# One pass over the weights for both column segments, three features held back, in a two-layer diffusion trunk

## The chip, the core and the metric

The kernel runs on one core of a Trainium2 chip. Its engines work side by side, each through its own queue in order: TensorE (matmuls; PE and, for its weight loads, PEld in the profile), VectorE (DVE), ScalarE (ACT), GpSimd (POOL) and SyncE (SP), which issues the DMAs. The metric is the time of one execution on the device, in microseconds (us), as the median of several runs.

## The reference

Two layers of a token mixer and a gated feed-forward network (FFN) over 512 latent tokens and 256 context tokens, all with 1024 features. The second layer needs the context only as keys and values.

```
for l in range(2):
    hl, hc = modulate(rmsnorm(xl), sh1, sc1) @ w_in[l], ...   # latent, context
    (four groups of heads: differential, windowed, neighbourhood attention, short convolution)
    xl = xl + g1 * (heads_l @ w_out[l])
    xl = xl + g2 * conv_ffn(modulate(rmsnorm(xl), sh2, sc2), w_up[l], ..., w_down[l])
    if l == 0:
        xc = xc + cg1 * (heads_c @ w_out[l])
        xc = xc + cg2 * conv_ffn(modulate(rmsnorm(xc), csh2, csc2), ...)
return rmsnorm(xl, final_norm_w)

conv_ffn: u = dwconv3(h @ w_up, conv_w) + conv_b;  g, v = split(u);  (silu(g) * v) @ w_down
```

All is float32. The kernel splits each operand of a matmul in a high part (rounded to the matmul's format) and a low part, the rest, and multiplies high by high, high by low and low by high: three matmuls for each tile of 128 input features.

## The kernel before

**Layout.** Features lie on the 128 partitions, in 8 tiles (`KT = 8`), tokens along the columns: 0 to 511 latent, 512 to 767 context. `x[m]` is the residual stream of feature tile m in SBUF, `y[k]` the normed input of the next product, with a high part `yh` and a low part `yl`. In layer 0 the two segments (`SEGS`) are the 512 latent and the 256 context columns; in layer 1, where the context is no longer needed, they are two halves (`HALVES`) of 256.

**Weights.** `prefetch` (L453) loads the next weight tiles in the order that `unit_order` (L433) yields, into 3 raw buffers; `split_weights` (L472) has ScalarE cast the high part (L481) and subtracts the low part (L486): on GpSimd in pieces of two tiles, or, with `fast`, the first five tiles on VectorE and the rest on GpSimd. There are two buffers for each part (`wh`, `wl`), and with `spare` two of another pool (`mrow`), which also takes the rows for the modulation sums of `mod_dve` (L304) during layer 0's FFN.

**The four stages that the change touches.** Stage 1 is layer 0's output projection with the norm before the FFN, stage 2 layer 0's last part of the down-projection (7 of 22 tiles) with the norm before layer 1's mixing, stage 3 and stage 4 the same two places of layer 1, where stage 4 ends in the final norm and the output. In each the weights are gone over twice, once for each segment: in `w_out` (L921) and in the loop over `sweeps` in `ffn` (L961). A product goes into one of two PSUM banks (`tp`), and VectorE adds it into x (`residual`, L914).

**The norm of a segment** is a generator: `rstd_steps` (L327) squares x on ScalarE and sums over features, then takes the root and the reciprocal, then spreads the result over all partitions by four small matmuls (`rb`, into the one PSUM bank tagged `pj`). For the second segment (`direct`) the sums over the eight tiles are made on TensorE, by matmuls with ones into the bank `pv` (`ms`); for the first, GpSimd and VectorE add the eight squares (L353) and TensorE sums once. Then `norm_apply` (L396) takes each feature tile k: VectorE multiplies x by the scale and by `rb`, straight from its bank (L404, called the first step below), ScalarE adds the shift and rounds to the high part (L408), and the low part is made on VectorE for even k (L414, the lower part) or on GpSimd for odd k (L410, L412).

**What sets the order.** A list scheduler orders each engine's instructions by its own estimate of when they are ready and by program order. `keep_in_program_order` pins an instruction behind the one traced just before it on its engine. `tick(n)` (L372) advances the norm in `self.pace` by n steps between the products of the other segment, and the first steps of features made under it are pinned (L406). `woven` (L379) runs the second segment's norm and, after each of its steps, one fill: products of the first segment with the weights of the two units that come next (`up_open`, or `early_start` in stage 2). While fills run, all of TensorE's matmuls are pinned, the broadcast of the root among them. The unit's results lie in the two `sc` tiles of PSUM.

In stage 1 the woven part is

```
first = [self.up_open(l, 0, gv, True) for gv in range(2)]
part = lambda u, k0, k1: lambda: self.up_product(u[1], u[0], y, a, b, range(k0, k1))
self.woven(steps, part(first[0], 0, 4), part(first[0], 4, 8), part(first[1], 0, 8))
```

so that the sums of the second norm come first, then half of unit 0, the last sum, the other half of unit 0, the broadcast, and unit 1.

After stage 2 the pools of the FFN are closed, and those of the mixing (`mixing_pools`, L249) take their memory; the first load into one of them is the table for the rotation (L588).

## Time and profile before

| what | value |
|---|---|
| median of 3 runs | 1758.03 us (1757.46 to 1758.92) |
| profiled execution: its time, its span | 1758.37 us, 1756.6 us |
| busy, share of the span: TensorE, its weight loads | 95%, 81% |
| VectorE, ScalarE, GpSimd | 54%, 46%, 57% |
| DMA moved | 244.15 MB, mean 139 GB/s |
| loads of w_out tiles, of w_down tiles of 448 KB, of 512 KB | 32, 48, 16 |

A busy share is a mean over stages with different limits, and TensorE's busy time counts matmuls that run slowly as busy. So the four stages are read one by one: how many matmuls fall in a stretch, what they take elsewhere, and what ended the waits. The window view gives, for a stretch, the busy time of each engine with its instructions, and the clock that was granted to TensorE as a share of 2.4 GHz.

### The profile page before, as it was taken

The numbers are of one execution on the slowest core, as the hardware profiler recorded it, in microseconds if no ns is written. First come the engines' busy times: TensorE is split into PE (matmuls) and PEld (weight loads), VectorE is DVE, ScalarE is ACT, GpSimd is POOL, SyncE is SP. The second block draws the span as 40 slices with busy tenths as digits, with TensorE's granted clock in tenths as the row PEclk, the third lists the DMA queues.
The fourth block names the chain that finished last, engine by engine and source line by source line (L and its number), as shares of the span: only waits on it lengthen the run. The fifth ranks groups of instructions, "written<-read, shape, count | busy, mean of one in ns | idle before, by whom it ended". The sixth has DMA issues, their size and how long they took to land. (4 is left out here: it accounts for less than half of the span.)

```text
span 1756.6 us, 26615 instructions
## 1 busy us (share of the span) xinstructions
PE 1672.1 (95%) x9740; PEld 1421.0 (81%) x9740; DVE 952.0 (54%) x1849; ACT 801.0 (46%) x1399; POOL 1002.0 (57%) x1348
## 2 busy tenths in 40 slices
PE   6899999899999999999999988999999999999997
PEld 4578878798878888888888877888879888888887
DVE  3577767562667754654355475877656422122245
ACT  4276766553443321332143354776654543242343
POOL 1424234776566654664467664434865776676763
PEclk9999999999999999999999999999999999999999
DMA  8566535336434433443333636453446323233334
GB/s 335 177 197 210 157 108 186 94 121 233 149 104 129 123 109 98 133 127 111 110 131 116 196 120 189 138 148 105 141 128 210 109 96 94 99 94 99 96 108 132
DMA packets 78450, 244.15 MB, mean 139 GB/s; under 512 B 9072, under 2 KB 12656, under 8 KB 78192
## 3 DMA queue, kind: packets, MB, share of 16 engines
q1 hardware_dynamic: 78320, 242.46, 43.6%
q8 instruction: 77, 1.26, 0.3%
q14 instruction: 53, 0.43, 0.1%
HBM read 214.64 MB, written 27.79 MB: 138 GB/s over the span
## 5 line engine op out<-in xcount | busy, mean ns | idle before, releaser
L486 POOL TENSOR_TENSOR wl<-raw,wh 128x256 fp32r<-128x256 f32 (+1 forms) x750 | 579.9, 803 | 556.1 <-ACT wh L481 528.5
L73 PE MATMUL pu<-y,wh 128*128 128x512 f32 (+1 forms) x1792 | 559.2, 388 | 4.2 <-DVE up L957 2.6
L481 ACT CAST wh<-raw 128x1024 fp32r<-128x1024 f32 (+1 forms) x228 | 233.6, 1027 | 353.8 <-PE pd L73 188.7
L73 PEld LDWEIGHTS pu<-y,wh 128*128 128x128 f32 x1792 | 331.8, 188 | 71.2 <-ACT wh L481 2.4
L73 PE MATMUL pu<-y,wl 128*128 128x512 f32 (+1 forms) x1072 | 369.0, 351 | 0.0
L73 PE MATMUL pj<-y,wh 128*128 128x512 f32 (+1 forms) x1216 | 325.4, 356 | 8.9 <-ACT ev L581 5.3
L73 PE MATMUL pd<-g,wh 128*128 128x512 f32 (+1 forms) x1048 | 290.2, 362 | 4.4 <-DVE x L917 2.8
L73 PEld LDWEIGHTS pj<-y,wh 128*128 128x128 f32 x1216 | 206.9, 192 | 39.1 <-ACT ev L581 8.2
L73 PEld LDWEIGHTS pu<-y,wl 128*128 128x128 f32 x1072 | 201.9, 188 | 31.1
L73 PEld LDWEIGHTS pd<-g,wh 128*128 128x128 f32 x1048 | 188.5, 193 | 34.2 <-ACT wh L481 4.0
L73 PE MATMUL pj<-y,wl 128*128 128x512 f32 (+1 forms) x608 | 212.0, 349 | 0.0
L954 DVE SCALAR_TENSOR_TENSOR up<-pu,par,up 128x511 f32<-128x511 f32 (+1 forms) x132 | 83.1, 658 | 231.4 <-ACT up L952 212.9
L73 PE MATMUL pd<-g,wl 128*128 128x512 f32 (+1 forms) x584 | 196.2, 342 | 2.9 <-DVE wl L486 2.8
L917 DVE SCALAR_TENSOR_TENSOR x<-pd,mod,x 128x256 f32<-128x256 f32 (+1 forms) x96 | 56.6, 592 | 168.9 <-PE pd L73 168.3
L73 PEld LDWEIGHTS pj<-y,wl 128*128 128x128 f32 x608 | 116.7, 192 | 14.5
L677 POOL TENSOR_TENSOR p<-p,rec 128x512 f32<-128x512 f32 (+2 forms) x80 | 79.5, 998 | 83.2 <-DVE rec L673 59.5
L73 PEld LDWEIGHTS pd<-g,wl 128*128 128x128 f32 x584 | 112.6, 193 | 17.3 <-DVE wl L486 3.5
L311 DVE SCALAR_TENSOR_TENSOR junk<-mrow,cbc 128x1024 f32<-128x1024 f32 x80 | 121.9, 1524 | 2.1 <-DMA mrow<-in_wmodt 1.3
L73 PE MATMUL po<-og,wh 128*128 128x256 f32 (+1 forms) x512 | 111.6, 314 | 3.9 <-ACT sq L344 2.5
L979 POOL TENSOR_TENSOR up<-up 128x256 f32<-128x256 f32 x105 | 105.3, 1028 | 1.4 <-DVE up L957 0.7
L748 DVE TENSOR_TENSOR wtl<-wtp,wth 128x512 fp32r<-128x512 f32 x132 | 87.4, 668 | 29.5 <-ACT wth L747 28.7
L73 PEld LDWEIGHTS po<-og,wh 128*128 128x128 f32 x512 | 84.8, 193 | 10.2 <-ACT sq L344 2.7
(174 smaller groups left out, 2370.8 us busy)
## 6 DMA issues: line engine op xcount, KB each, us to landing
raw<-in_wup SPq DMA_DIRECT2D x88, 512.0 KB, 3.4
mrow<-in_wmodt SPq DMA_DIRECT2D x56, 512.0 KB, 3.7
raw<-in_win SPq DMA_DIRECT2D x44, 512.0 KB, 3.6
raw<-in_wdn SPq DMA_DIRECT2D x48, 448.0 KB, 3.3
mraw<-in_wmod SPq DMA_DIRECT2D x40, 512.0 KB, 7.2
raw<-in_wout SPq DMA_DIRECT2D x32, 512.0 KB, 3.5
qk<-hl SPq DMA_DIRECT2D x16, 768.0 KB, 3.6
stk<-qk SPq DMA_DIRECT2D x32, 384.0 KB, 5.4
```

Of the source, the lines that this page charges most:

```text
L73: i = self.nc.tensor.matmul(out, **kw)
L311: self.tc.keep_in_program_order(nc.vector.scalar_tensor_tensor(out=junk, in0=raw, scalar=1.0, in1=self.cbc[:, i], op0=ALU.mult, op1=ALU.mu ...
L481: i = nc.scalar.copy(out=wh, in_=raw)
L486: eng.tensor_tensor(out=wl[:, a:b], in0=raw[:, a:b], in1=f32v(wh[:, a:b]), op=ALU.subtract)
L677: self.nc.gpsimd.tensor_tensor(out=p, in0=p, in1=r.broadcast_to(list(p.shape)), op=ALU.mult)
L748: nc.vector.tensor_tensor(out=wl[:, :n * 256], in0=tp[:, :n * 256], in1=f32v(wh[:, :n * 256]), op=ALU.subtract)
L917: self.nc.vector.scalar_tensor_tensor(out=x[m][:, a:b], in0=p[:, c:c + n], scalar=gate[:, m, (0 if b <= SEQ else 1):(1 if b <= SEQ else 2) ...
L954: nc.vector.scalar_tensor_tensor(out=u[:, a + 1:b], in0=p[:, a:b - 1], scalar=cw[:, 0:1], in1=u[:, a + 1:b], op0=ALU.mult, op1=ALU.add)
L979: eng.tensor_tensor(out=uv[:, a:b], in0=ug[:, a:b], in1=uv[:, a:b], op=ALU.mult)
```

## The change

`HELD = 3`. Each of the four stages goes over its weights once (`sweep`). For the first five feature tiles both segments are multiplied right away: in layer 0 as 512 and 256 columns, in layer 1 as one product of all 512. For the last three only the first segment is, and the weights are kept (the last tile's in the spare buffers). Then the first segment's norm starts, and the three held products of the second segment follow, with one step of the norm after each. Then the second segment's squares and sums are traced, then the next two units are opened (their weights split), then the rest of the first norm (`tick(KT + 2)`). The second norm is woven with fills of one feature tile each, for both units in turn. Both norms sum on TensorE (`direct` is True) and put their broadcast in `pj`. `norm_apply` takes one tile and returns its lower part as a function, which `norm_steps` calls two tiles later; under `tick` the lower parts are pinned too. All other stages are as before; the opening norm of the kernel calls the lower parts after each pair of tiles. In stage 2 the eight stores of x for layer 1 (L236) are traced after the early products instead of between the passes.

```diff
@@ -190,22 +192,21 @@
                 i = nc.sync.dma_start(out=x[m][:, :NT], in_=xsrc[:, m, :NT])
                 if m == 0:
                     tc.keep_in_program_order(i)
-            y = None
-            for sg in segs:
-                self.w_out(l, s, x, sg)
-                y = y or self.new_y()
-                steps = self.norm_steps(x, y, sg, self.affn[l], self.mod[l][:, 24:32], sg != segs[0])
-                if sg == segs[0]:
-                    self.pace = steps
-                    self.tick(1)
-            first = [self.up_open(l, 0, gv, True) for gv in range(2)]
+            y = []
+
+            def norm(sg, l=l, x=x, y=y, segs=segs):
+                y.extend([] if y else self.new_y())
+                return self.norm_steps(x, y, sg, self.affn[l], self.mod[l][:, 24:32], True, "pj")
+
+            steps, first = self.sweep(lambda m: ("wout", l, m), "po", s, x, self.mod[l][:, 16:24], segs, norm,
+                                      lambda: [self.up_open(l, 0, gv, True) for gv in range(2)])
             a, b = segs[0]
-            part = lambda u, k0, k1: lambda: self.up_product(u[1], u[0], y, a, b, range(k0, k1))
-            self.woven(steps, part(first[0], 0, 4), part(first[0], 4, 8), part(first[1], 0, 8))
+            part = lambda k: lambda: [self.up_product(u[1], u[0], y, a, b, range(k, k + 1)) for u in first]
+            self.woven(steps, *[part(k) for k in range(KT)])
             a, b = segs[1]
             self.pin = ALL
             for u in first:
-                part(u, 0, 8)()
+                self.up_product(u[1], u[0], y, a, b)
             self.pin = None
             todo = []
             if need:
...
@@ -216,29 +217,30 @@
 
-            def after(sg, l=l, need=need, x=x, y2=y2):
-                if need:
-                    if not y2:
-                        self.scale_vec(l + 1, self.amix[l + 1], O_NM, 8)
-                        y2.extend(self.new_y())
-                    steps = self.norm_steps(x, y2, sg, self.amix[l + 1], self.mod[l + 1][:, 0:8], sg != segs[0])
-                    if sg == segs[0]:
-                        self.pace = steps
-                        self.tick(1)
-                    else:
-                        early = self.early_start(l + 1, True)
-                        part = lambda n, k0, k1: lambda: self.early_products([early[n]], y2, SEGS[0], range(k0, k1))
-                        self.woven(steps, part(0, 0, 4), part(0, 4, 8), part(1, 0, 8))
-                        self.early_products(early[1:], y2, SEGS[1], range(KT))
-                        self.split_weights(spare=True)
-                    if sg[1] <= SEQ:
-                        for k in range(KT):
-                            nc.sync.dma_start(out=xd[:, k, sg[0]:sg[1]], in_=x[k][:, sg[0]:sg[1]])
-                else:
-                    self.pace = self.final(x, sg, sg != segs[0])
-                    self.tick(1 if sg == segs[0] else 99)
-
-            self.ffn(l, x, y, segs, first, todo, after)
+            def norm(sg, l=l, need=need, x=x, y2=y2, segs=segs):
+                tag = "pj"
+                if not need:
+                    return self.final(x, sg, True, tag)
+                if not y2:
+                    self.scale_vec(l + 1, self.amix[l + 1], O_NM, 8)
+                    y2.extend(self.new_y())
+                return self.norm_steps(x, y2, sg, self.amix[l + 1], self.mod[l + 1][:, 0:8], True, tag)
+
+            opening = lambda l=l, need=need: self.early_start(l + 1, True) if need else None
+
+            def after(steps, early, need=need, x=x, y2=y2):
+                if not need:
+                    for _ in steps:
+                        pass
+                    return
+                part = lambda k: lambda: self.early_products(early, y2, SEGS[0], [k])
+                self.woven(steps, *[part(k) for k in range(KT)])
+                self.early_products(early[1:], y2, SEGS[1], range(KT))
+                self.split_weights(spare=True)
+                for k in range(KT):
+                    nc.sync.dma_start(out=xd[:, k, :SEQ], in_=x[k][:, :SEQ])
+
+            self.ffn(l, x, y, segs, first, todo, norm, opening, after)
             y = y2
         fes.close()
 
...
@@ -363,11 +365,18 @@
                     rhs=r[:, :w], start=True, stop=True)
         return rb
 
-    def norm_steps(self, x, y, sg, A, sh, direct=False):
-        r = yield from self.rstd_steps(x, *sg, direct)
+    def norm_steps(self, x, y, sg, A, sh, direct, tag):
+        r = yield from self.rstd_steps(x, *sg, direct, tag)
+        held = []
         for k in range(KT):
-            self.norm_apply(x, y, sg, A, sh, r, [k])
+            low = self.norm_apply(x, y, sg, A, sh, r, k)
+            held.append(low)
+            if k > 1 and held[k - 2]:
+                held[k - 2]()
             yield
+        for f in held[-2:]:
+            if f:
+                f()
 
     def tick(self, n):
 
...
@@ -393,32 +402,38 @@
-    def norm_apply(self, x, y, sg, A, sh, r, ks):
+    def norm_apply(self, x, y, sg, A, sh, r, k):
+
         nc = self.nc
         a, b = sg
         n = b - a
         j = 0 if b <= SEQ else 1
-        for k in ks:
-            t = self.u.tile([128, T], F32, tag="u", name="yt")
-            yh, yl, _ = y[k]
-            i = nc.vector.scalar_tensor_tensor(out=t[:, :n], in0=x[k][:, a:b], scalar=A[:, k, j:j + 1],
-                                               in1=r[:, :n], op0=ALU.mult, op1=ALU.mult)
+        t = self.u.tile([128, T], F32, tag="u", name="yt")
+        yh, yl, _ = y[k]
+        i = nc.vector.scalar_tensor_tensor(out=t[:, :n], in0=x[k][:, a:b], scalar=A[:, k, j:j + 1],
+                                           in1=r[:, :n], op0=ALU.mult, op1=ALU.mult)
+        if self.ticking:
+            self.tc.keep_in_program_order(i)
+        nc.scalar.activation(out=yh[:, a:b], in_=t[:, :n], func=AF.Identity, bias=sh[:, k, j:j + 1])
+        if self.slow and k % 2:
+            nc.gpsimd.tensor_tensor(out=t[:, :n], in0=t[:, :n],
+                                    in1=sh[:, k, j:j + 1].broadcast_to([128, n]), op=ALU.add)
+            nc.gpsimd.tensor_tensor(out=yl[:, a:b], in0=t[:, :n], in1=f32v(yh[:, a:b]), op=ALU.subtract)
+            return None
+
+        def low():
+            i = nc.vector.scalar_tensor_tensor(out=yl[:, a:b], in0=t[:, :n], scalar=sh[:, k, j:j + 1],
+                                               in1=f32v(yh[:, a:b]), op0=ALU.add, op1=ALU.subtract)
             if self.ticking:
                 self.tc.keep_in_program_order(i)
-            nc.scalar.activation(out=yh[:, a:b], in_=t[:, :n], func=AF.Identity, bias=sh[:, k, j:j + 1])
-            if self.slow and k % 2:
-                nc.gpsimd.tensor_tensor(out=t[:, :n], in0=t[:, :n],
-                                        in1=sh[:, k, j:j + 1].broadcast_to([128, n]), op=ALU.add)
-                nc.gpsimd.tensor_tensor(out=yl[:, a:b], in0=t[:, :n], in1=f32v(yh[:, a:b]), op=ALU.subtract)
-            else:
-                nc.vector.scalar_tensor_tensor(out=yl[:, a:b], in0=t[:, :n], scalar=sh[:, k, j:j + 1],
-                                               in1=f32v(yh[:, a:b]), op0=ALU.add, op1=ALU.subtract)
...
@@ -918,15 +930,38 @@
                                                 scalar=gate[:, m, (0 if b <= SEQ else 1):(1 if b <= SEQ else 2)],
                                                 in1=x[m][:, a:b], op0=ALU.mult, op1=ALU.add)
 
-    def w_out(self, l, s, x, sg):
-        a, b = sg
+    def sweep(self, unit, name, ops, x, gate, segs, norm, opening, todo=()):
+
+
+
+        whole = segs if segs[1][1] == T else SEGS[:1]
+
+        def one(m, w, a, b):
+            p = self.bank("tp", name)
+            self.product(p[:, :b - a], w, ops, a, b)
+            self.residual(p, x, gate, m, a, b)
+
+        kept = []
         for m in range(KT):
-            w = self.weights(("wout", l, m), b - a == 256, m % 3 == 2 and l == 0)
-            p = self.bank("tp", "po")
-            self.product(p[:, :b - a], w, s, a, b)
-            self.residual(p, x, self.mod[l][:, 16:24], m, a, b)
-            self.tick(2 if m < 3 else 1)
-        self.tick(KT)
+            w = self.weights(unit(m), spare=m == KT - 1)
+            if m < KT - HELD:
+                for a, b in whole:
+                    one(m, w, a, b)
+            else:
+                one(m, w, *segs[0])
+                kept.append((m, w))
+            if todo and m % 2:
+                todo.pop(0)()
+        self.pace = norm(segs[0])
+        self.tick(1)
+        for m, w in kept:
+            one(m, w, *segs[1])
+            self.tick(1)
+        steps = norm(segs[1])
+        next(steps)
+        opened = opening()
+        self.tick(KT + 2)
+        return steps, opened
 
 
     def up_open(self, l, i, gv, fast=False):
...
@@ -988,25 +1023,21 @@
                     ug = gate_unit(i + 1)
                 if todo:
                     todo.pop(0)()
-            sweeps = [[sg] for sg in segs] if k1 == NF else [cseg]
-            for sweep in sweeps:
-                for m in range(KT):
-                    w = self.weights(("wdn", l, m, k0, k1), sweep[0][1] - sweep[0][0] == 256,
-                                     k1 == NF and m % 3 == 2 and l == 1)
-                    for a, b in sweep:
-                        p = self.bank("tp", "pd")
-                        if k1 < NF and a == SEQ:
-                            self.product2(p, w, G, a, b)
-                            self.residual(p, x, gate, m, a, b, 2)
-                        else:
-                            self.product(p[:, :b - a], w, G, a, b)
-                            self.residual(p, x, gate, m, a, b)
-                    if todo and m % 2:
-                        todo.pop(0)()
-                    self.tick(2 if m < 3 else 1)
-                self.tick(KT)
-                if k1 == NF:
-                    after(sweep[0])
+            if k1 == NF:
+                after(*self.sweep(lambda m: ("wdn", l, m, k0, k1), "pd", G, x, gate, segs, norm, opening, todo))
+                continue
+            for m in range(KT):
+                w = self.weights(("wdn", l, m, k0, k1))
+                for a, b in cseg:
+                    p = self.bank("tp", "pd")
+                    if a == SEQ:
+                        self.product2(p, w, G, a, b)
+                        self.residual(p, x, gate, m, a, b, 2)
+                    else:
+                        self.product(p[:, :b - a], w, G, a, b)
+                        self.residual(p, x, gate, m, a, b)
+                if todo and m % 2:
+                    todo.pop(0)()
 
 
 class Group:
```

## Rows read from the trace of the kernel before

**Rows 1.** Stages' windows: us, busy time and (instructions) by engine, granted clock, DMA.

```profile
core 0: us, PE busy (x) PEld busy (x) DVE busy (x) ACT busy (x) POOL busy (x), PEclk, DMA share, GB/s
410.00:440.00 30.00, 30.00 (x134) 24.88 (x133) 5.33 (x7) 9.54 (x12) 21.55 (x26) 1.00 0.48 175
1335.00:1345.00 10.00, 10.00 (x86) 10.00 (x84) 5.60 (x9) 5.29 (x8) 7.21 (x8) 1.00 0.59 175
446.47:476.69 30.22, 27.03 (x225) 25.90 (x223) 23.92 (x29) 17.33 (x26) 21.32 (x15) 0.94 0.34 110
476.69:495.25 18.56, 18.56 (x137) 15.45 (x136) 9.53 (x17) 10.39 (x16) 7.82 (x11) 1.00 0.43 170
1009.09:1041.18 32.09, 26.94 (x241) 25.18 (x240) 24.80 (x34) 18.44 (x28) 21.45 (x17) 0.89 0.41 123
1041.18:1056.66 15.48, 15.48 (x95) 13.03 (x89) 8.12 (x16) 5.29 (x12) 9.62 (x13) 1.00 0.29 99
1056.66:1070.68 14.02, 10.08 (x51) 8.79 (x49) 8.02 (x10) 2.40 (x4) 10.35 (x13) 0.88 0.49 172
1320.23:1370.39 50.16, 47.60 (x406) 46.21 (x404) 33.12 (x48) 26.52 (x43) 33.53 (x28) 1.00 0.62 193
1371.09:1387.00 15.91, 13.89 (x119) 12.88 (x113) 8.97 (x16) 6.69 (x14) 9.71 (x13) 1.00 0.21 67
1698.08:1746.47 48.39, 46.20 (x386) 44.03 (x384) 27.46 (x44) 20.98 (x33) 20.16 (x19) 0.96 0.46 137
465.50:473.50 8.00, 5.45 (x46) 5.06 (x44) 6.31 (x9) 2.81 (x6) 7.11 (x6) 0.79 0.42 131
```

**Rows 2.** TensorE in order of time: start, us, line, operation, out<-in, shape, count, wait before.

```profile
451.59 0.42 PE L73 MATMUL ms<-sq,ones 128*32 128x128 f32 x8
...
476.69 0.77 PE L73 MATMUL ms<-sq,ones 128*32 128x64 f32 x40
477.39 0.72 PE L73 MATMUL pu<-y,wh 128*128 128x512 f32 x2
...
483.46 1.00 PE L73 MATMUL rb<-rstd,ident 128*128 128x64 f32 x8
484.27 0.71 PE L73 MATMUL pu<-y,wh 128*128 128x512 f32 x2
...
1066.22 0.50 PE L73 MATMUL pj<-y,wh 128*128 128x256 f32 x2 [3.94 <-ACT ev L581]
```

**Rows 3.** All engines in order of time, at the end of the kernel.

```profile
456.73 3.38 DVE L404 SCALAR_TENSOR_TENSOR yt<-x,affn,rb 128x512 f32<-128x512 f32 x5 [0.41 <-PE rb L73]
460.76 1.79 DVE L414 SCALAR_TENSOR_TENSOR y<-yt,mod,y 128x512 fp32r<-128x512 f32 x1
463.52 1.44 DVE L414 SCALAR_TENSOR_TENSOR y<-yt,mod,y 128x512 fp32r<-128x512 f32 x1
470.95 0.74 DVE L414 SCALAR_TENSOR_TENSOR y<-yt,mod,y 128x512 fp32r<-128x512 f32 x1
484.57 2.44 DVE L404 SCALAR_TENSOR_TENSOR yt<-x,affn,rb 128x256 f32<-128x256 f32 x6 [2.93 <-PE rb L73]
486.92 2.48 DVE L414 SCALAR_TENSOR_TENSOR y<-yt,mod,y 128x256 fp32r<-128x256 f32 x3
```

**Rows 4.** VectorE in order of time, first and second norm of stage 1.

```profile
1746.57 0.48 DVE L917 SCALAR_TENSOR_TENSOR x<-pd,mod,x 128x256 f32<-128x256 f32 x1 [2.46 <-PE pd L73]
1747.62 0.32 PE L73 MATMUL ms<-sq,ones 128*32 128x64 f32 x8 [0.61 <-ACT sq L344]
1748.35 0.55 DVE L358 RECIPROCAL rstd<-rstd 128x64 f32<-128x64 f32 x1 [1.29 <-ACT rstd L357]
```

**Rows 5.** Groups by line and shape: busy us, mean ns, idle before.

```profile
L311 DVE SCALAR_TENSOR_TENSOR junk<-mrow,cbc 128x1024 f32<-128x1024 f32 x80 | 121.9, 1524 | 2.1 <-DMA mrow<-in_wmodt 1.3
L412 POOL TENSOR_TENSOR y<-yt,y 128x512 fp32r<-128x512 f32 x8 | 13.7, 1712 | 0.4
```

**Rows 6.** SyncE's queue in order of time, end of stage 2.

```profile
1056.29 0.33 SPq L588 DMA_DIRECT2D rope<-in_rope  x1
```

22 lines of the change are left out of this document (11 added, 11 removed).

## The prediction

> **What bounds the kernel now.** Times are read in this order: the window table, the matmul engine's order of time, then VectorE's. TensorE sets the pace almost everywhere, so what counts is where it runs slower than its own rate. That rate stands in two undisturbed windows: 133 weight loads in 30.00 us, so 0.2256 us for a 512-column matmul, and 84 in 10.00 us, so 0.119 us for a 256-column one [rows 1]. A group of sums costs 0.42 us alone at 128 columns, 0.14 at 64 columns in a run of five (40 records from 476.69 to 477.39), and a broadcast of the root 0.81 (483.46 to 484.27) [rows 2].
>
> Four stages of the kernel are touched. In each I subtract from the window's length what its matmuls need at these rates, and call the rest lost [rows 1].
> - Stage 1 (layer 0, w_out): the second pass takes 30.22 us for 192 x 0.119 = 22.85 and 1.5 of sums and broadcast: 5.85 lost. The opening of the FFN takes 18.56 for 48 x 0.2256 + 16 x (0.2256 + 0.119) + 1.76 = 18.1: 0.45 lost. Together 6.3. Of this, 1.7 is the clock: behind a wait, in the 8 us from 465.5, the mean granted clock is 0.79, part of it at 1.2 GHz instead of 2.4, and 8 x 0.21 = 1.7 us of full speed are missing.
> - Stage 2 (layer 0, last w_down): 32.09 us for 168 x 0.119 = 20.0 and 2.1: 10.0 lost. The opening takes 15.48 for 14.75: 0.7. The next 14.02 hold 24 x (0.2256 + 0.119) = 8.27, so 5.75 are lost there, 3.94 of them in one wait for ScalarE's evacuation at 1066.22 [rows 2].
> - Stage 3 (layer 1, w_out): 50.16 us for 372 x 0.119 = 44.27 and 1.4: 4.5 lost. The opening takes 15.91 for 12.5: 3.4, of which I leave 0.6 (the eviction of the first unit, unchanged). Together 7.3.
> - Stage 4 (layer 1, last w_down): 48.39 us for 336 x 0.119 = 40.0 and 2.0: 6.4 lost, with a mean clock of 0.96.
>
> **The change part by part.** *One pass, weights read once.* 32 loads, 32 casts and 32 subtractions go. TensorE never worked on them, so their price is the lost time above: a second pass of 256 columns uses up a weight in 2.5 to 2.9 us, while VectorE's part alone was queued behind and among the norm's work. In the new pass a feature lasts 24 x (0.2256 + 0.119) = 8.3 us in stage 1, and only three 256-column products without new weights are left over. I take all the losses above as removed in stages 1 to 4 (6.3, 10.7, 7.3, 6.4), but put back 0.5 in each of stages 1 to 3 and 0.7 in stage 4 for small waits that stay. In stage 4 the first product now takes 512 columns, so the last g is needed 18 x 0.2256 = 4.1 us after the start instead of 2.1, and VectorE's part of a weight no longer stands in front of it.
>
> *Halves joined in layer 1.* Five features take one 512-column product in place of two of 256: 2 x 0.119 - 0.2256 = 0.0125 us for each of 5 x 24 and 5 x 21 products: 1.5 us in stage 3, 1.3 in stage 4. On this the Trainium skill ("TensorE: Matmul & The Clock Gate", Back-to-back issue gap) has a smaller gain: its gap is columns / 2.4 plus 2.5 ns, so joining two halves saves 2.6 ns, an estimate of 0.6 us for the 225 products; by it the sum below would be 2.2 us higher. The rows decide for 0.0125.
>
> *Sums of the first norm on TensorE.* Seven more groups in each stage, on the path. In stages 3 and 4 these are 64 columns: 7 x 0.14 = 1.0 us. In stages 1 and 2 they are 128 columns, for which no run of groups is shown: between 1.0 and 7 x 0.42 = 2.9; I take 1.65, nearer to the 64-column run, since these too stand in a row. GpSimd's and VectorE's additions go; they cost only by delaying what is in the losses.
>
> *The new order at the joint.* This is the term that decides. In the code, each first step of the norm on a feature is pinned behind the VectorE instruction traced just before it. The steps after the held products are: feature 0 after the held product 6, feature 1 behind the residual of held product 7, then 2, lower part 0, 3, 4, lower 2, 5, 6, lower 4, 7, lower 6. So at the end of the last held product VectorE still has the residual, seven first steps and the lower parts to do. On TensorE the pinned order is: sums of the second norm, part 0 of both units, **the second norm's broadcast**, part 1 and so on. Both norms' broadcasts use the one bank with the tag pj. The second can't be written before feature 7 of the first norm has read it. Before, eight times 0.2256 x 3 us of products stood between, and the first norm had been done in the second pass. Now there is one part of 6 matmuls.
>
> Priced in stage 1 from the end of the last held product: the last sum is through at 1.27 (residual, square, group: 1746.57 to 1747.62, plus 0.22) [rows 3]. The residual ends at 0.43; a first step of 512 columns takes 0.66 (five in 3.38); a lower part takes 0.74 with GpSimd quiet (470.95) and 1.44 to 1.79 with it at work (463.52, 460.76) [rows 4]; I take 1.4, because GpSimd has the odd features to do all that time. Lower part 0 ends at 0.43 + 2 x 0.66 + 1.4 = 3.15; TensorE waits 1.9, then does part 0 (6 x 0.2256 = 1.35) to 4.5. Feature 7 is at 3.15 + 5 x 0.66 + 2 x 1.4 = 9.25, and the second reciprocal, 0.55 [rows 3], falls in between: 9.85. TensorE waits 5.35. Together 7.25. Bounds: with lower parts of 0.74 it is 5.2; with 1.79, and the reciprocal behind the last lower part, 10.5. The idle stretch should take the clock down once, as 465.5 to 473.5 shows: 1.7.
> Stage 2 is the same plus one product of the modulation row on VectorE (1.4 of the mean 1.52 [rows 5]): its row buffer is taken by the spare weights of feature 7 until the last held product. So 8.65, and 1.7.
> Stage 3 has 256 columns: first steps 0.41 (six in 2.44), lower parts 0.83 (three in 2.48) [rows 4]. Lower part 0 ends at 2.1, part 0 of 0.72 at 2.8, feature 7 with the reciprocal at 6.35: waits of 0.8 and 3.55, 4.4 together, and 1.7 for the clock. Bounds 3.1 and 5.2.
> Stage 4 has no pins on its output steps and no parts behind; the tail after the last product stays as it is (the remaining 0.7 above covers an output step in front of a residual).
>
> *What lies behind stage 2.* The wait of 3.94 at 1066.22 ends a chain that starts with the rope table, issued at 1056.29 right when the norm's buffers come free [rows 6]: 9.9 us from issue to the end of the wait. With the new order TensorE gets there 31.6 us after the last held product (sums 1.27, waits 8.65, clock 1.7, part 0 1.35, broadcast 0.81, seven parts 9.5, the second segment 2.9, the next unit 5.4). The broadcast is through at 12.1, VectorE's eight steps and four lower parts for the second segment take 8 x 0.41 + 4 x 0.83 = 6.6, GpSimd's last feature 0.8 more, so the norm ends at 19.5 and the chain at 29.4. So the 5.75 lost there go, though no edit touches them. The cover for that: the eight stores of x (256 KB each) now stand behind the norm in program order on SP's queue. Their data is ready before the held products, about 10 us earlier than the last of these ends; if they are issued only behind the norm, the buffers come free later, and up to 5.75 stay. The modulation row's load, which waits for its buffer on the same queue, has the same price.
>
> **The two units in turn** and the **lower parts two behind** add no instruction (nor does the same order in the opening norm, which runs in the first 110 us under the modulation's loads); they make TensorE use up a feature in 1.35 us instead of 0.68, and that holds GpSimd's odd features (1.71 for the second of two steps [rows 5]) in time once the broadcast is through.
>
> Sum: stage 1: -6.3 + 0.5 + 1.65 + 7.25 + 1.7 = +4.8. Stage 2: -10.7 + 0.5 + 1.65 + 8.65 + 1.7 - 5.75 = -3.95. Stage 3: -7.3 + 0.5 - 1.5 + 1.0 + 4.4 + 1.7 = -1.2. Stage 4: -6.4 + 0.7 - 1.3 + 1.0 = -6.0. Together -6.4. The profiled execution took 1758.37 us (its span 1756.6), 0.34 above the median of 1758.03; so 1752.0 against it, 1751.6 against the median. I say **1752**.
>
> **The rivals.**
> - *The broadcast doesn't hold TensorE up.* If VectorE gets through the first norm under the held products, the waits (20.3) and the clock (5.1) go: 1752 - 25 = 1727. For it: three held products are 8.6 us, more than one norm's chain needs to its first feature. Against: the pins, and the single bank. Chance 0.1.
> - *VectorE is not slowed by GpSimd.* Lower parts at 0.74 and 0.41: waits of 5.2, 6.6 and 3.1, 5.4 us less, and one clock drop less: 1745. Chance 0.2.
> - *Slower: the chain on VectorE is long.* GpSimd works on odd features while each lower part wants to start, and the second reciprocal lands behind lower part 6. At 1.79 and 0.83 the waits are 10.5, 11.9 and 5.2 (7.3 more), and each takes the clock down twice as long (+5.1; stage 2 now has a mean of 0.89 over 32 us, 3.5 missing): 1764. It decides once the broadcast comes more than 12 us after the last held product in stage 1. The Trainium skill ("SBUF — State Buffer", Who interferes with whom) goes further: a VectorE instruction with two SBUF inputs and a GpSimd one that reads SBUF block each other for the whole instruction, so that each lower part could wait out a whole GpSimd step. With the row of 1.71 for one [rows 5] a lower part would be 2.45, the three before feature 7 add 3.2 us a 512-column stage, and the time would be about 1759. Rows of 1.44 to 1.79 show part of it. Chance 0.2.
> - *The lost time wasn't the weights'.* The waits in stages 2 and 4 then stay (5.75 behind stage 2, 1.7 of clock in stage 4): 1759.5, no change. Chance 0.15.
>
> **How the numbers follow.** My forecast has 0.35, and half of its spread of 4 us lies inside no change. A run of this kernel can tell about 0.2%, or 3.5 us, from no change. Faster by more: 0.1 + 0.2 + most of 0.35 = 0.57. Within it: 0.15 and a bit of the forecast: 0.22. Slower: 0.21. The range goes from 1739 (the short bounds with all losses gone) to 1764 (the slower rival) and leaves out the first rival and worse than the third.
>
> **What would show it.** In the changed kernel's trace TensorE's broadcast before part 1 must wait for VectorE's first step of feature 7 by about 5 us in stages 1 and 2 and 3.5 in stage 3; the granted clock must fall right there. The second-pass waits for split weights must be gone, the 3.94 at the evacuation too, and stage 4 must run from its first product to its last in 42 us instead of 48.4. If the broadcast doesn't wait, I am wrong by tens of microseconds; if the waits of stage 4 stay, by six.

## The result and the profile after

| kernel | median | ratio to the kernel before |
|---|---|---|
| before | 1758.47 us (1757.46 to 1760.38) | 1 |
| changed | 1781.80 us (1780.97 to 1784.43) | 1.0128, 95% interval 1.0111 to 1.0144 |

The change makes the kernel slower by 1.28%, some 23 us. The forecast was 1752 us, 1739 to 1764; both the sign and the range are wrong. (In the section on the rows, the fences under Rows 3 and Rows 4 stand under each other's headings; the prediction refers to the headings.)

What it set out to save, it saves. From the page of the changed kernel: busy time, data moved, the casts of weights (228 before, 196 now).

```profile
PE 1692.0 (95%) x9739; PEld 1419.3 (80%) x9739; DVE 890.4 (50%) x1783; ACT 773.8 (43%) x1369; POOL 957.0 (54%) x1344
...
DMA packets 73840, 228.41 MB, mean 128 GB/s; under 512 B 8560, under 2 KB 12144, under 8 KB 73584
...
L493 ACT CAST wh<-raw 128x1024 fp32r<-128x1024 f32 (+1 forms) x196 | 202.3, 1034 | 326.8 <-PE pd L74 183.2
```

Where the time went, in the window view of the changed kernel (columns as in [rows 1]): four features of stage 1's pass; stage 1 and stage 2 from the last held product to the end of the opening; what follows up to the first scores; stage 3, from 3 us behind its first product, with its opening; stage 4.

```profile
411.61:447.18 35.57, 35.57 (x213) 30.34 (x213) 5.09 (x9) 8.21 (x11) 14.08 (x20) 1.00 0.32 112
475.20:507.02 31.82, 24.06 (x152) 18.96 (x152) 16.13 (x28) 17.49 (x29) 17.00 (x18) 0.79 0.18 64
1046.95:1077.50 30.55, 23.50 (x155) 18.30 (x154) 18.95 (x32) 13.38 (x27) 21.83 (x28) 0.72 0.27 86
1077.50:1098.57 21.07, 15.15 (x80) 12.26 (x79) 9.02 (x11) 6.58 (x10) 9.97 (x11) 0.99 0.60 167
1341.19:1410.95 69.76, 66.41 (x500) 57.73 (x499) 23.46 (x44) 26.22 (x49) 33.88 (x46) 0.95 0.30 99
1722.06:1767.11 45.05, 44.54 (x305) 37.06 (x304) 10.39 (x17) 13.84 (x24) 17.77 (x28) 1.00 0.16 50
```

The same work before: stage 1's opening 18.56 [rows 1], stage 3 with its opening 66.77 and stage 4 48.39 [rows 1], and for stage 2 and what follows, in the kernel before:

```profile
1038.61:1056.66 18.05, 16.49 (x135) 13.78 (x135) 8.61 (x17) 6.95 (x14) 11.62 (x15) 1.00 0.30 96
1056.66:1078.85 22.19, 16.68 (x81) 13.80 (x79) 9.14 (x12) 6.18 (x10) 13.16 (x17) 0.92 0.68 202
```

With the passes themselves (first to last product: stage 1 75.2 to 73.7, stage 2 with the FFN ahead of it 543.3 to 539.9) the difference of the spans, 22.6, is made up like this:

| stretch | forecast | found |
|---|---|---|
| stage 1: pass, opening | +4.8 | -1.5, +13.3 |
| stage 2: pass, opening, to the scores | -3.95 | -3.4, +12.5, -1.1 |
| stage 3: pass, opening | -1.2 | -2.1, +5.1 |
| stage 4 | -6.0 | -3.3 |
| behind the last product, all the rest | 0 | +2.0, +1.1 |

So the loss is at the openings, above all the two of layer 0, and the passes are shorter by less than forecast. TensorE at the openings of layer 0, in order of time:

```profile
476.46 0.93 PE L74 MATMUL ms<-sq,ones 128*32 128x64 f32 x24 [0.82 <-ACT sq L346]
480.73 0.44 PE L74 MATMUL ms<-sq,ones 128*32 128x64 f32 x8 [3.34 <-ACT sq L346]
...
482.33 1.22 PE L74 MATMUL pu<-y,wh 128*128 128x512 f32 x2
...
488.37 1.94 PE L74 MATMUL rb<-rstd,ident 128*128 128x64 f32 x8 [3.11 <-DVE rstd L360]
490.07 1.20 PE L74 MATMUL pu<-y,wh 128*128 128x512 f32 x2
...
1055.06 0.80 PE L74 MATMUL pj<-y,wh 128*128 128x512 f32 x1 [1.92 <-DVE y L425]
...
1061.01 1.94 PE L74 MATMUL rb<-rstd,ident 128*128 128x64 f32 x8 [3.44 <-DVE yt L413]
1062.71 1.20 PE L74 MATMUL pj<-y,wh 128*128 128x512 f32 x2
...
1083.81 0.50 PE L74 MATMUL pj<-y,wh 128*128 128x256 f32 x2 [0.69 <-ACT ev L593]
...
1098.60 1.62 PE L74 MATMUL sca<-stk 128*128 128x512 f32 x4 [5.22 <-DMA stk<-qk]
```

These rows show three things: the broadcast does hold TensorE up, as forecast, but by 3.11 and 3.44 and not by 5 (in stage 3 by 2.18 and not by 3.5); in stage 1 other waits, for squares on ScalarE, stand ahead of it; and each broadcast and each pair of products around it takes about double what it took before (1.94 against 1.00, 1.20 against 0.71 [rows 2]), since the granted clock is at 1.2 GHz, half of full speed, for 13.65, 17.07 and 6.83 us in the stages 1 to 3. The window view of these stretches:

```profile
480.49:494.14 13.65, 9.82 (x48) 7.36 (x49) 10.71 (x18) 9.47 (x19) 12.02 (x11) 0.50 0.04 17
1050.51:1067.58 17.07, 11.23 (x58) 8.06 (x59) 14.09 (x23) 8.28 (x17) 14.80 (x14) 0.50 0.17 58
1395.26:1402.09 6.83, 6.42 (x30) 6.45 (x31) 5.10 (x11) 3.01 (x7) 5.32 (x9) 0.50 0.01 2
```

Behind stage 2 the wait of 3.94 for the evacuation [rows 2] is down to 0.69, but the one at the scores, 5.22 now, was 1.54 in the kernel before:

```profile
1078.84 0.94 PE L73 MATMUL sca<-stk 128*128 128x512 f32 x4 [1.54 <-DMA stk<-qk]
```

Why the squares come late in stage 1: ScalarE in order of time.

```profile
477.04 1.28 ACT L217 ACT_TABLE_LOAD   x1
478.46 1.91 ACT L217 ACTIVATE cbc<-cbc 128x2048 f32<-128x2048 f32 x1
...
483.76 1.28 ACT L359 ACT_TABLE_LOAD   x1
```

The Silu of the modulation vector, which ran behind the root before, now runs in the middle of the second norm's squares, with a table load of its own and one more for the root. In stage 2 it is VectorE that stands still (order of time):

```profile
1052.09 1.42 DVE L313 SCALAR_TENSOR_TENSOR junk<-mrow,cbc 128x1024 f32<-128x1024 f32 x1 [2.64 <-DMA mrow<-in_wmodt]
...
1060.13 0.73 DVE L413 SCALAR_TENSOR_TENSOR yt<-x,amix,rb 128x512 f32<-128x512 f32 x1
```

The modulation row can only be loaded when the spare weights have freed its buffer (its load is issued at 1047.87), and the pinned first steps stand behind it; the last of them ends at 1060.86, and the broadcast can start.

### The profile page after: what moved, and what is told of

It is laid out like the page before. It is cut to its first block, busy times and chain, and to the rows that moved or that the text cites. A ratio compares the mean times of both kernels' runs of the same rounds, so it can differ in the third digit from the quotient of the medians.

```text
span 1779.2 us, 26279 instructions
## 1 busy us (share of the span) xinstructions
PE 1692.0 (95%) x9739; PEld 1419.3 (80%) x9739; DVE 890.4 (50%) x1783; ACT 773.8 (43%) x1369; POOL 957.0 (54%) x1344
## 4 chain that ended last, share of the span: by engine, by line
PE 82%; DVE 6%; DMA 4%; ACT 4%; issue 2%; POOL 1%; SPq 1%; DVEq 0%; ACTq 0%; POOLq 0%
PE pu L74 34%; PE pd L74 16%; PE pj L74 14%; PE po L74 6%; PE pv L74 3%; DMA stk<-qk 3%; PE wtp L78 2%; PE scc L74 1%; ACT p L677 1%; PE scb L74 1%; DVE nm L669 1%; PE sca L74 1%; PE rb L74 1%; POOL wl L498 1%; PE ms L74 1%
## 5 line engine op out<-in xcount | busy, mean ns | idle before, releaser
L498 POOL TENSOR_TENSOR wl<-raw,wh 128x256 fp32r<-128x256 f32 (+1 forms) x766 | 561.8, 765 | 615.4 <-ACT wh L493 588.6
L493 ACT CAST wh<-raw 128x1024 fp32r<-128x1024 f32 (+1 forms) x196 | 202.3, 1034 | 326.8 <-PE pd L74 183.2
L74 PE MATMUL pd<-g,wh 128*128 128x512 f32 (+1 forms) x978 | 282.7, 371 | 2.1 <-DVE x L929 0.8
L74 PEld LDWEIGHTS pd<-g,wh 128*128 128x128 f32 x978 | 176.0, 188 | 35.2 <-issue 1.6
L74 PE MATMUL pd<-g,wl 128*128 128x512 f32 (+1 forms) x549 | 187.9, 349 | 0.1
L929 DVE SCALAR_TENSOR_TENSOR x<-pd,mod,x 128x512 f32<-128x512 f32 (+1 forms) x91 | 55.7, 614 | 205.4 <-PE pd L74 204.8
L74 PEld LDWEIGHTS pd<-g,wl 128*128 128x128 f32 x549 | 103.4, 188 | 16.2 <-POOL wl L498 1.0
L74 PE MATMUL po<-og,wh 128*128 128x256 f32 (+1 forms) x432 | 106.7, 338 | 0.1
L78 PE MATMUL wtp<-ident,p 128*128 128x128 f32 x512 | 84.7, 277 | 6.9 <-DVE p L1126 3.5
```

The costliest lines, as they stand in the source:

```text
L74: i = self.nc.tensor.matmul(out, **kw)
L78: i = self.nc.tensor.transpose(out, in_, self.ident)
L493: i = nc.scalar.copy(out=wh, in_=raw)
L498: eng.tensor_tensor(out=wl[:, a:b], in0=raw[:, a:b], in1=f32v(wh[:, a:b]), op=ALU.subtract)
L929: self.nc.vector.scalar_tensor_tensor(out=x[m][:, a:b], in0=p[:, c:c + n], scalar=gate[:, m, (0 if b <= SEQ else 1):(1 if b <= SEQ else 2) ...
```

## The experiments

Unless said otherwise an experiment is the changed kernel with one edit. Ratios are to the kernel before, which ran beside each, with 95% intervals; the changed kernel has 1.0128 (1.0111 to 1.0144).

### Undoing the first norm's sums on TensorE

```diff
-return self.norm_steps(..., True, "pj")
+return self.norm_steps(..., sg != segs[0], "pj")      # the same in stage 2 and in final
```

> The changed kernel (1781.8 us, 1.0128 of the kernel before) with one edit: the first norm's squares added up on GpSimd and VectorE again. Theory R (the groups stand in TensorE's way one for one, also on one pass): seven lone groups of 0.35 us less in each of the stages, 2.1 to 2.5 us each, 1772 to 1775 us, 1.007 to 1.009. Rival (on one pass TensorE's order around the last products is set by the first norm's chain, and an addition of some 1 us on VectorE behind the last square makes that chain longer by as much as the groups gave): 1.011 to 1.013.

Measured: 1.0027 (1.0017 to 1.0038), 1763.8 us. This one part accounts for four fifths of the loss, twice what theory R expected. The windows of this kernel for the same four features of stage 1 and for stage 4:

```profile
410.65:444.12 33.47, 33.47 (x193) 29.63 (x193) 4.84 (x8) 7.99 (x10) 19.07 (x24) 1.00 0.33 113
1711.21:1753.31 42.10, 41.37 (x249) 35.83 (x247) 10.84 (x19) 13.85 (x24) 21.24 (x33) 1.00 0.17 52
```

33.47 against 35.57 for four features, so 0.53 us for each lone group of 128 columns, and 42.10 against 45.05 in stage 4, 0.42 in the mean for each of seven groups of 64 (two of that norm's eight are split up there, and they stand in nine places). One group of 128 columns in the changed kernel, and the same place without it:

```profile
419.93 0.28 PE L74 MATMUL po<-og,wl 128*128 128x256 f32 x1
420.14 0.41 PE L74 MATMUL ms<-sq,ones 128*32 128x128 f32 x4
420.48 0.72 PE L74 MATMUL po<-og,wh 128*128 128x512 f32 x2
421.05 0.40 PE L74 MATMUL po<-og,wl 128*128 128x512 f32 x1
```

```profile
418.98 0.28 PE L74 MATMUL po<-og,wl 128*128 128x256 f32 x1
419.10 0.63 PE L74 MATMUL po<-og,wh 128*128 128x512 f32 x2
419.57 0.39 PE L74 MATMUL po<-og,wl 128*128 128x512 f32 x1
```

From one low product's start to the next is 1.12 us with the group and 0.59 without: the group itself shows 0.34, and the products on both sides of it lose another 0.2. The Trainium skill ("TensorEngine Tiling (Array Packing)", Key Properties) says that changing the tiling mode drains TensorE; the sums are matmuls of 32 output partitions between ones of 128, so a lone group changes it twice, and the rows agree with a loss of 0.1 us on either side; that the drain is what costs it, no run here shows by itself. A run of five groups, the row that the forecast used, has little of that: 0.14 each [rows 2].

### Undoing one pass

In part: five tiles' weights are fetched and cast a second time, behind the three held ones (the edit in short).

```diff
+REDO = 5
+for m in held + range(KT - HELD - REDO, KT - HELD):   # second segment; weights anew for the last five
```

> The changed kernel with one pass undone in part: the weights of five of the eight tiles are fetched and cast a second time for the second segment, behind the three held ones; all other parts of the change stay (early sums, lower parts two tiles behind, both units in turn, sums on TensorE). Theory J (one pass costs the cover: the first norm's chain of some 18 us had 25 us of second-segment products beside it and has 9 us now): the waits for the first norm vanish, the first product of stage 1 and of stage 2 follows the last held product within 3 us, and with three weights in hand the time lost to weights in the second pass is smaller than before: 1750 to 1758 us. Theory K (the other parts of the change cost it): the stages stay 3 us or more each behind those of the kernel before, 1768 to 1778 us.

Measured: 1.0053 (1.0041 to 1.0065), 1769.4 us, in theory K's range. Stage 2's opening is back to 15.3 us (from the last product at 1048.03 to the end of the 48 products of both units at 1063.34; 15.2 before, 27.8 in the changed kernel), so J's mechanism holds, but only 13 of the 23 us come back, and the second pass of stage 2 has a wait of 4.6 us for a low weight. Wholly: `HELD = 0`, `REDO = 8`, spare buffers and the split of the weights as in the kernel before.

> The change without its one pass: the weights are fetched and cast twice for all eight tiles, none is held, and the second segment takes them in the order of the kernel before; what stays of the change is the sums on TensorE for both norms, the early sums of the second norm, the lower parts two tiles behind, and the units in turn. Theory J (one pass with too little cover is the cause): 1756 to 1762 us, as the kernel before (1758). Theory K (the rest of the change costs of its own, as the 11 us suggest by which the run with five tiles fetched twice stays behind the kernel before): 1765 to 1772 us.

Measured: 1.0041 (1.0029 to 1.0053), 1765.5 us. Theory K: the other parts cost something of their own, and the second pass of stage 2 still waits for low weights, 3.9 us in three waits, as VectorE's order of time in that kernel shows (weights are the `wl` lines):

```profile
1026.49 1.40 DVE L414 SCALAR_TENSOR_TENSOR yt<-x,amix,rb 128x512 f32<-128x512 f32 x2
1027.81 1.61 DVE L499 TENSOR_TENSOR wl<-raw,wh 128x640 fp32r<-128x640 f32 x1
...
1031.53 1.83 DVE L426 SCALAR_TENSOR_TENSOR y<-yt,mod,y 128x512 fp32r<-128x512 f32 x1
1033.28 1.66 DVE L499 TENSOR_TENSOR wl<-raw,wh 128x640 fp32r<-128x640 f32 x1
```

Which of the other parts it is, four runs over two passes were to tell, each with one more part undone: the turn of the units, the delayed lower parts, the first norm's sums, the early sums.

> Over two passes (the run without one pass, 1765.5 us, 1.0041 of the kernel before), with the turn of the two units undone. Theory E (the turn delays the first unit's evacuation and the chain to the scores): the wait at the scores of stage 2 falls, 1.000 to 1.002 of the kernel before. Theory P (over two passes the turn costs nothing, the loss is in the second pass): 1.003 to 1.005.

> Over two passes, with each lower part right behind its first step again. Theory Q (the delayed lower parts come between VectorE's low weights in the second pass, which TensorE waits for by 2.28 and 1.24 us in stage 2): these waits go, 1.001 to 1.003 of the kernel before. Rival (a lower part waits for ScalarE in VectorE's queue if it is not behind, which was the reason to delay it): the waits stay or grow, 1.004 to 1.006.

> Over two passes, with the squares of the first norm added up on GpSimd and VectorE again instead of lone groups of sums on TensorE (0.34 to 0.36 us a group, seven groups in each of four stages, some 9.8 us less the 0.7 us for the one group at the end). Theory R (the groups stand in TensorE's way one for one): stages 1 to 4 each get 1 to 2 us shorter, 1.000 to 1.001 of the kernel before. Rival (they fill time in which TensorE waits for weights anyway, and the additions would take GpSimd and VectorE from the weights): 1.003 to 1.006.

> Over two passes, with the early sums of the second norm undone. On one pass that edit cost 10 us, since the sums then wait behind the whole first norm. Over two passes the first norm is over by then: theory S: within 0.1% of 1.0041. Rival (the order of squares ahead of the first units' weights on ScalarE is the loss): 1.002.

Measured: 1.0052 (1.0040 to 1.0064), 1.0046 (1.0034 to 1.0058), **0.9967** (0.9955 to 0.9979), 1.0046 (1.0033 to 1.0059). Three can't be told from the run without these edits; so theory Q falls, and P and S stand. The sums alone decide, again by more than R expected (12 us). The third, 1753.5 us, beats both kernels. Four kernels make the main table:

| first norm's sums | one pass | two passes |
|---|---|---|
| on TensorE | 1.0128 | 1.0041 |
| added on GpSimd and VectorE | 1.0027 | 0.9967 |

The sums cost 1.0% on one pass and 0.7% on two; one pass costs 0.9% with them and 0.6% without. Neither pays. Together they cost more than the change loses, since what is left of it without both is 0.3% faster than the kernel before; which of its other parts gains that was not tested.

### The other parts of the change, on one pass

The units one behind the other again, so that 12 products of unit 0, not 6 of both, stand ahead of the broadcast:

```diff
-self.woven(steps, *[part(k) for k in range(KT)])
+self.woven(steps, part(first[0], 0, 4), part(first[0], 4, 8), part(first[1], 0, 8))
```

> The changed kernel with the turn of the two units undone: behind the sums stand 12 matmuls of the first unit, then 12 more, then the second unit's 24, as in the kernel before. Theory E (two units in turn delay the end of the first unit, and with it in stage 2 the first evacuation and the chain from it to the scores, whose wait of 5.2 us at 1092.99 is new): stage 2 ends 4 to 5 us earlier, stages 1 and 3 the same; 1777 us. Theory F (the parts in turn cost nothing and save waits: 12 matmuls ahead of the broadcast need four first steps and lower parts instead of one): the broadcast comes later by the time to y 3, but it is the same chain that ends last; within 2 us of 1781.8 or slower by up to 5 us.

Measured: 1.0088 (1.0075 to 1.0101), 1775.0 us. The turn costs 0.4% on one pass (over two, above, nothing). But not as theory E had it: the wait at the scores is still 5.1 us, though the first unit's evacuation comes at 1062.60 instead of 1074.14. The gain is at the openings (3.4 us in stage 1, 2.2 up to the scores in stage 2, 2.9 in stage 3): more products lie ahead of the broadcast, and no wait for it is left in stage 2. From the waits view of this kernel, 1042 to 1098 (who waited for whom: us, times, longest):

```profile
PE sca L74 <- DMA stk<-qk: 5.1, 1, 5.1
PE pj L74 <- POOL y L421: 3.2, 2, 2.0
PE pj L74 <- DVE y L425: 1.9, 1, 1.9
...
```

The early sums undone (no `next(steps)` ahead of the opening):

> The changed kernel with the early sums undone: the squares of the second norm come behind the first norm's steps, so the first steps on VectorE no longer wait for the six buffers that the squares hold. Theory G (the early squares take the buffers and ScalarE from the first norm: first steps at 1053.44 instead of about 1049.4, 2.7 to 4 us of VectorE idle in stages 1 and 2): the first product starts earlier by the 7.1 us and 3.7 us of waiting sums in stages 1 and 2, and the stages end 3 to 4 us earlier each; about 1774 us. Theory H (the second norm is what ends last; later sums move its broadcast back by as much): the parts of the first norm finish earlier, but TensorE then waits for the second norm's broadcast and first steps; 1781 to 1788 us.

Measured: 1.0188 (1.0173 to 1.0203), 1792.1 us: theory H, and worse; in stage 1 TensorE waits 10.9 us for squares, 9.1 of them at once. The early sums are worth 10 us on one pass.

### Taking away one wait

The second broadcast in the bank of the sums (`tag = "pv"` for the second segment):

> The changed kernel (1781.8 us) with one edit: the second norm's broadcast takes the PSUM bank of the sums instead of the bank in which the first norm's broadcast is still being read. Theory A (the shared bank with the pinned order holds TensorE): in stage 2 the broadcast no longer waits for the last first step (end 1060.86) but for the reciprocal (1056.91), and part 1 then for its GpSimd lower part (1058.62), so part 1 starts about 4 us earlier than 1062.71 and stage 2 ends 4 to 5 us earlier; stage 3 gains about 2 us; in stage 1 the broadcast waited for the reciprocal (488.22) and not for the bank (487.76), so at most 0.5 us there. Sum 1774 to 1776 us. Theory B (the bank is only the last to be seen; the parts wait for the chain of first steps and lower parts on VectorE and GpSimd in any case): the broadcast's wait moves to the parts behind it, the end of the held-up part 7 stays within 1 us, 1780 to 1782 us.

Measured: 1.0118 (1.0103 to 1.0133), not to be told from the changed kernel. The trace shows both theories half right. The broadcast no longer waits, and the second part of stage 2 (TensorE in order of time, below) starts 12.1 us behind the last product instead of 15.9:

```profile
1055.89 1.81 PE L74 MATMUL rb<-rstd,ident 128*128 128x64 f32 x8
1057.46 1.20 PE L74 MATMUL pj<-y,wh 128*128 128x512 f32 x2
```

The parts behind it follow without a wait, so first steps and lower parts did not pace them. But at the scores the wait grows from 5.2 to 7.7 us, and 2.7 of the 3.8 us are given back: the scores start 50.6 us behind the last product instead of 51.7.

The Silu held in its place in the program, behind the norm:

```diff
-nc.scalar.activation(out=self.cbc, in_=self.cbc, func=AF.Silu)
+tc.keep_in_program_order(nc.scalar.activation(out=self.cbc, in_=self.cbc, func=AF.Silu))
```

> The changed kernel with one edit: the Silu of the modulation vector (1.91 us, with a table load of 1.28 us ahead of it and one of 1.28 us behind it, at 477.04 to 485.04) is held in its place in the program, behind the second norm, instead of in the gap of stage 1. Theory C (ScalarE's Silu holds the squares, they the sums, and so the rest of stage 1): the first product of stage 1 starts about 4 us earlier than 482.33 and the broadcast's end moves from 490.07 to about 486; stage 1 loses 4 us less, 1778 us. Theory D (VectorE's and GpSimd's first steps and lower parts set when the parts can run; the Silu only fills a wait that is there anyway): the first product moves, but the end of the last part of stage 1 moves by under 1 us; 1781 to 1782 us. The stages 2 to 4 are the same under both.

Measured: 1.0116 (1.0102 to 1.0129). Stage 1's first product moves from 7.3 to 3.9 us behind the last pass, and the end of the opening by as much (3.5 us), as theory C has it. Then 1.6 us are lost again: behind a wait for VectorE's `up` (2.1 us, in both kernels) the granted clock falls to 1.2 GHz for 3.41 us at 506.34, in this run and not in the changed kernel's. About 2 us are left in the trace, within the intervals.

All lower parts on VectorE (`if False:` in place of `if self.slow and k % 2:`):

> The changed kernel (1781.8 us) with one edit: all lower parts on VectorE, none on GpSimd. Theory I (GpSimd's chain of odd lower parts, add 1.04 us and subtract 1.71 us each, is what ends last in stage 2: the load of the rope table is issued at 1071.59, right at the end of GpSimd's last lower part at 1071.56, and the scores wait for what follows it): the rope load comes 3 to 6 us earlier, VectorE's lower parts take 0.74 us instead of up to 1.76, and the time falls to 1775 to 1778 us. Theory B (VectorE is the bound): VectorE gets 8 more instructions a norm pair, 4 of about 0.75 and 4 of about 0.48 us, the second norm's broadcast, which waits for the last first step, comes 2 to 4 us later in the stages 1 to 3, 1787 to 1792 us.

Measured: 1.0118 (1.0100 to 1.0136), between the two. The broadcast of stage 2 waits 4.5 instead of 3.4 us for the last first step, the rope table's load is issued at 1072.23 instead of 1071.59, and VectorE's lower parts fall from 884 to 639 ns in the mean of both shapes. By this run neither engine's share of the lower parts is the bound by itself.

Products that nothing reads, in the waits of stages 1 and 2:

```diff
+for _ in range(n):   # 2 behind each of seven groups of sums, 12 ahead of the broadcast; all pinned
+    self.mm(out, lhsT=self.identr, rhs=self.maskb[:, :256], start=True, stop=True)
```

> The changed kernel with added TensorE work that nothing reads, in the stages 1 and 2 only: two products of 256 columns behind each of seven groups of the second norm's sums, and twelve ahead of its broadcast. It fills the time in which TensorE waits. Theory L (the waits cost twice: TensorE's clock falls to 1.2 GHz in them, at 480.49 for 13.65 us and at 1050.51 for 17.07 us, and the broadcast and the parts behind it then take double): the clock stays up or falls later, the broadcast takes 0.81 instead of 1.70 us and the 42 products behind it 9.5 instead of 11.8 us, stages 1 and 2 lose 2.5 to 4 us less each, 1774 to 1777 us. Theory B (the parts behind the broadcast are paced by first steps and lower parts, and the clock only stretches waits): the time stays within 1.5 us, or grows by up to 3 us where the added work stands in the way.

Measured: 1.0112 (1.0096 to 1.0127). The clock does stay up longer (means of 0.86 and 0.87 from the last held product to the end of the 48 parts, against 0.74 and 0.69), and these stretches shrink from 26.4 to 23.6 and from 27.7 to 26.2, though TensorE does more in them (window view, first the changed kernel, then this one):

```profile
475.20:501.62 26.42, 18.66 (x121) 14.25 (x121) 15.56 (x26) 15.27 (x26) 16.01 (x16) 0.74 0.22 78
1046.95:1074.62 27.67, 20.62 (x130) 15.42 (x129) 17.52 (x29) 13.26 (x27) 19.94 (x21) 0.69 0.26 82
```

```profile
474.20:497.84 23.64, 21.10 (x147) 16.64 (x147) 15.84 (x26) 15.28 (x26) 16.43 (x16) 0.86 0.23 87
1044.80:1071.01 26.21, 23.15 (x156) 18.13 (x155) 17.64 (x29) 13.32 (x27) 19.89 (x21) 0.87 0.21 70
```

This is theory L's mechanism, but below its size (2.8 and 1.5 us, where it has 2.5 to 4 each): 4.2 us in the trace, not certain in the medians.

### What ends stage 2

Three edits (bank, Silu, units one behind the other) together on one pass:

> One pass with three held, as in the changed kernel (1781.8 us), and three edits together that were measured one by one: the second broadcast in the bank of the sums (2.8 us by the medians), the Silu behind the second norm (3.2 us), the units one behind the other (6.8 us). Theory N (each takes away a wait of its own): the gains add, 1769 us. Theory I (stage 2 ends by the load of the rope table, which waits for the last lower part of the second norm, and the scores start 24 to 27 us behind it in every run so far: 22.6 us in the kernel before, 27.0 in the changed one, 25.4 and 25.5 in the runs with the bank and with the units): the gains of the bank and the units don't add in stage 2, 1771 to 1775 us.

Measured: 1.0100 (1.0086 to 1.0113), no better than the units alone. A fourth edit puts the rope table into memory shared with VectorE's unread products, so that its load waits for no first step or lower part:

```diff
-tab = self.cb.tile([128, 2, SEQ], F32, tag="rope", bufs=1, name="rope")
+tab = self.wp.tile([128, 2, SEQ], F32, tag="rope", bufs=1, name="rope")   # junk of mod_dve takes the same tag
```

> The run with three edits on one pass, and a fourth: the rope table is loaded into memory that is shared with VectorE's unread products of the modulation instead of memory that the first steps and lower parts use, so that its load waits for none of them. Theory I: rotating starts as soon as the evacuations are there, the scores of stage 2 start 4 to 6 us earlier than in the run with three edits, 1765 to 1769 us. Theory O (the lower parts stand in GpSimd's queue ahead of the rotation's product anyway, so an earlier table waits there): 0 to 1 us less than the run with three edits.

Measured: 1.0083 (1.0069 to 1.0097), 1772.4 us, between the two theories; the interval overlaps that of the run with three edits. The traces are plain. SyncE's order and the waits view, for the changed kernel, the run with three edits, and this one:

```profile
1071.59 0.33 SPq L600 DMA_DIRECT2D rope<-in_rope  x1
```

```profile
1068.75 0.33 SPq L600 DMA_DIRECT2D rope<-in_rope  x1
...
PE sca L74 <- DMA stk<-qk: 5.5, 1, 5.5
```

```profile
1049.42 0.33 SPq L600 DMA_DIRECT2D rope<-in_rope  x1
...
PE sca L74 <- DMA stk<-qk: 1.2, 1, 1.2
```

The load is issued 19 us earlier and the wait goes from 5.5 to 1.2, as theory I has it. What bank and units gained in stage 2 was lost to that load. The same edit on the kernel before:

> The kernel before (1758.5 us) with one edit: the rope table in the memory of VectorE's unread products, as above. In that kernel the table's load is issued at 1056.29, right behind the second norm's lower parts, and TensorE stands still for 3.94 us at 1066.22 for an evacuation that waits behind the rotation. Theory I: the rotation starts up to 6 us earlier, that wait and part of the scores' wait go, 1752 to 1755 us. Theory O: GpSimd and VectorE reach the rotation no earlier than now, 1757 to 1759 us.

Measured: **0.9977** (0.9966 to 0.9988), 1753.9 us: faster than both kernels, in theory I's range; the wait of 3.94 for the evacuation [rows 2] is down to 0.7, the scores' wait of 1.54 is gone, and the scores start 3.9 us nearer to stage 2's last product. (In the run that was profiled, 1756.8 us and one of the longer ones, 3.8 us are lost again between the scores and stage 3, so the gain as a whole rests on the medians.)

### Combinations

> The second fetch of five tiles' weights as in the run with that edit alone, with three more: the second broadcast in the bank of the sums, the Silu behind the second norm, and the two units one behind the other as in the kernel before. Theory J: with the cover back these three find little left to save: 0 to 4 us below the run with the second fetch alone, 1747 to 1757 us. Theory M (they are worth what they were worth alone, 2.8, 3.2 and 6.8 us against the changed kernel): 8 to 13 us below it, 1740 to 1748 us.

Measured: 1.0053 (1.0039 to 1.0066), the same as the second fetch alone; theory J: with the cover back, the three edits find no wait.

> Two passes, additions for the first norm (the run that came out at 0.9967 of the kernel before), and the rope table in the memory of VectorE's unread products (0.9977 alone on the kernel before). Theory N (each takes away a wait of its own): 0.994 to 0.995, some 1748 us. Rival (with the units in turn the first evacuation comes later, so the table's load is not what the rotation waits for): 0.996 to 0.997.

Measured: 0.9978 (0.9968 to 0.9988), 1754.2 us. The two gains don't add, and the interval overlaps that of either edit alone. The traces show why: over two passes the table's load doesn't hold TensorE up. The waits at the evacuation and at the scores are 0.7 and 2.1 us with this edit (load issued at 1007.3) and 0.7 and 2.3 without it (1046.9).

## Why the prediction was wrong

The steps that failed are three terms of the sum: the sums of the first norm on TensorE, 5.3 us forecast and 13.3 found; the clock at the joint, 5.1 forecast and some 13.7 found; and what lies behind stage 2, where 5.75 were to be gained and 1.1 were.

**The saving by one pass was right.** Stage 4 was to run in 42.4 us, 1.0 of it for lone sums; without these it takes 42.10, at a clock of 1.00, so the rest is off by 0.7. Without them the four passes are 6.0, 6.3, 5.0 and 6.3 us shorter than before, 23.6 in all, where the forecast comes to some 26. No wait for `wl` is left in the changed kernel's four stages, and one of 0.5 for `wh`.

**The sums on TensorE were mis-sized**, 5.3 us in the sum. They took 0.53 and 0.42 us a group, not 0.24 and 0.14: 7 x 0.53 x 2 + 7 x 0.42 x 2 = 13.3, and the passes of the kernel without them are shorter by 4.5, 3.1, 3.0 and 2.95, together 13.6. The value was taken from the row of a run of groups, though the text had the lone group of 0.42 for 128 columns as its upper bound, and the change itself puts the groups one by one behind each feature. Even the bound left out what the neighbours lose.

**The joint** was the right place: the broadcast waits where it was said to. The waits ahead of it come to 7.75, 7.05 and 2.87 us in the stages 1 to 3, against 7.25, 8.65 and 4.4, and that the sum is so near is in part luck, for other waits are in it. In stage 1 4.6 us are for the second norm's own squares, for which ScalarE's queue had not been gone through; in stage 2 the row for the modulation was foreseen as 1.4 us of work, not as a wait of 2.64 ahead of it. The lower parts were 0.65 to 1.76 us, 1.08 in the mean, so the 1.4 taken for them was high; the rule of the Trainium skill ("SBUF — State Buffer", Who interferes with whom), by which they would be 2.45, goes further than these rows.

What was mis-sized at the joint is the **clock**, put at 1.7 a stage for one drop. It stayed down for 13.65, 17.07 and 6.83 us, with the waits inside or just ahead of these stretches, and TensorE was at work for 9.82, 11.23 and 6.42 of them. Half of this work is what full speed would have saved, an estimate: 4.9, 5.6 and 3.2, together 13.7 against 5.1. The products put into the waits gave back 4.2 us of it.

**Behind stage 2** the 5.75 us did leave the place where they were, and 1.1 us of them was gained: the chain from the rope table moves with the second norm's end, since its load still waits for that norm's buffers, and it ends at the scores instead of the evacuation. The text had worked out that the chain would end 2 us before TensorE needs it; it had the norm ending 19.5 us behind the last held product, and the load was issued at 24.6 (1071.59). The eight stores of x that it feared were not in the way: the last is issued at 1039.30.

**The slower rival** had the sign, and its point of decision, a broadcast later than 12 us behind the last held product of stage 1, was passed (475.20 to 490.07, 14.9 us). But its mechanism, lower parts of 1.79 us and waits of 10.5, 11.9 and 5.2, did not come true; only its longer clock drops did (10.2 us, 13.7 found). That its 1764 lies nearer to the result is luck.

**What adds up.** Forecast and trace are 29.0 us apart (-6.4 and +22.6). The sums make up 8.0 of it, the clock 8.6, the place behind stage 2 4.6, the passes without sums some 2, what lies behind the last product 2.0 (all eight sums of the second norm stand there now) and the rest of the kernel 1.1; the waits take off 2.6. Some 5 us are put down to no row. (In the prediction 9.25 and 0.55 make 9.80, not 9.85; nothing hangs on it.)

**The units in turn**, costed at nothing, cost 7 us on one pass: they halve the work that stands ahead of the broadcast. Over two passes nothing of this shows: in that run TensorE doesn't wait for the second broadcast of stage 2 at all.
